# Output projection of a decoder trunk: six of eight tiles as three Strassen pairs with factors through DRAM, tiles 6 and 7 plain and last

## The chip, the cores and the metric

The kernel runs on one core of a Trainium2 chip. The core has five engines that run their own instruction streams and meet at semaphores: TensorE (PE in the profile; PEld is its weight load), VectorE (DVE), ScalarE (ACT), GpSimd (POOL) and SyncE (SP). SP, ACT and POOL also issue DMAs. Data lie in SBUF (128 partitions) and, for matmul results, in PSUM (eight banks of 128 x 512 floats). The metric is the device time of one execution in microseconds (us), the median of several runs.

## The reference

A sequence of 1024 positions with model width 1024 goes through one RG-LRU layer and one attention layer, both with a residual, and a final norm. The change lies in the end of the attention layer:

```
def mla_layer(x, norm_g, w_in, q_norm, w_uq, w_out, k_nope, k_rope, v, cos, sin):
    ...
    o = causal_block_attention(q_nope, q_rope, k_nope, k_rope, v)
    y = o.reshape(bsz, seq, N_HEADS * V_DIM) * jax.nn.silu(gate)
    return y @ w_out
...
x = x + mla_layer(...)
return rms_norm(x, final_norm)
```

There are 8 heads of 128 values, so `y` is 1024 x 1024 and `y @ w_out` is a product of two 1024 x 1024 matrices. Everything is float32.

## The kernel before

**Layout.** Activations lie transposed: 128 channels on the partitions, 1024 positions in the free dimension. A *page* is one such 128 x 1024 tile; a pool of 36 pages (`pgs`, `NPAGES`) serves nearly all large tiles, and an allocation waits until a page is free. A product in float32 accuracy is made of three matmuls on split operands: `hl` (lines 83 to 85) writes the high part on ACT and the remainder on DVE, and `mm3` (lines 115 to 118) issues high x high, high x low and low x high.

**Order.** The code is traced in program order and a list scheduler puts the instructions of each engine in order when the program is built, by priority and by what is ready in its model (`tc.high_priority` raises a block's priority). On the chip each engine then runs its stream strictly in that order.

**Strassen pairs that exist already.** The in-projection of the attention layer (`pair`, lines 628 to 667) multiplies two output tiles at a time in seven products of four k-pieces in place of eight (Strassen's scheme in Winograd's form), on factors of the activations that `factors` (line 510) makes and combinations of weight blocks from `wpair` (line 535). The last two of its pairs run just ahead of attention.

**Attention** (lines 989 to 1026) loops over 8 heads and, in each, 8 query blocks of 128 rows. `scores` (line 890) makes the scores of a block two blocks ahead (`LOOK`), with mask, row maximum (line 908), exponential (911), reciprocal (912) and, on DVE, the multiply by that reciprocal (913). `transposes` (916) turns the block's weights on PE and splits them. `pv` (927) multiplies four blocks with the values, multiplies the result with the gate on DVE (line 940) and splits it into the head's two pages `ysb`. For heads 0 to 5 (`NSPILL`) these pages are spilled to DRAM (line 946, GpSimd's DMA queue) and loaded again by `yload` during the last head. Between blocks, other work is put in by hand-written tables: key and query projections of the next head (`KQ_AT`), values (`V_AT`), and in the last head the first parts of the output projection (`D_AT`, `dpart`): tiles 0 and 1 for the first 512 columns and heads 0 to 5, 12 parts of three matmuls.

**Output projection and final norm** (lines 1034 to 1103). `wout` (960) loads the weights of a tile, high part by a casting DMA on GpSimd's queue and remainder on DVE. Then for each of three column chunks of 512, 256 and 256 (`CHUNKS`) the eight tiles follow one another, each with 24 matmuls (`mmt`), an addition of the residual from DRAM (`x1d`, line 1081), a square on ACT (1086) and its sum on DVE (151). After the second tile of the next chunk, `final` (1048) ends the chunk before: a matmul with ones sums the squares over partitions, `root` (1043) makes the reciprocal root, and DVE multiplies each tile by gain and root and sends it out. The last chunk gets its gains on ACT (1094) and ends with four DVE multiplies of two tiles each and four output DMAs (1100 to 1103).

Of the kernel before, what the change touches and what calls it, by code (L numbers as in the profile page):

```python
# [27 lines left out]
NSPILL = 6  # L28
WPRI = 100
WOUT_AT = (-1, 1, 2)  # L30
YL_AT = (0, 0, 0, 0, 1, 2)
DSTART = 0
DPART = tuple((dt, k, k + 1) for dt in range(2) for k in range(6))
# [6 lines left out]
D_AT = (0, 4, 1, 1, 1, 0, 3, 2)  # L40
# [7 lines left out]
FINAL = ((0, 2, "sync"), (2, 4, "scalar"), (4, 6, "sync"), (6, 8, "scalar"))  # L48
# [11 lines left out]
def trunk(tc, xT, wina, vecs, wgate, wouta, winc, wuk, wuv, wuq, wuqr, woutb, rope, outT):  # L60
# [746 lines left out]
    for j in range(0, NH, 2):  # L807
        gts = [[tk(), tk()] for _ in range(2)]
        w = wpair(6 + j, wa)
        if j < NH - 2:  # L810
            banks = four()
        else:

            pp.close()
            pss = es.enter_context(tc.tile_pool(name="pss", bufs=2, space=PSUM, reuse_waits="tile"))
            banks = [pss.tile([P, HW], F32, tag="pm", bufs=4, name=nm("pm")) for _ in range(4)]
# [16 lines left out]
    def pm():  # L833
        return pss.tile([P, HW], F32, tag="pm", bufs=4, name=nm("pm"))
# [55 lines left out]
    def scores(hd, qb, k, q, qs):  # L890
# [5 lines left out]
        sc = ps[:, o:o + nk]  # L896
        for c0, c1 in ((0, min(nk, HW - o)), (HW - o, nk)):
            if c0 >= c1:
                continue
            c = slice(c0, c1)  # L900
            T.matmul(out=sc[:, c], lhsT=q[0][:, ql], rhs=k[0][:, c], start=True, stop=False)  # L901
            T.matmul(out=sc[:, c], lhsT=q[0][:, ql], rhs=k[1][:, c], start=False, stop=False)  # L902
            T.matmul(out=sc[:, c], lhsT=q[1][:, ql], rhs=k[0][:, c], start=False, stop=False)  # L903
            T.matmul(out=sc[:, c], lhsT=qs[:, ql], rhs=R1[:, c], start=False, stop=False)  # L904
            T.matmul(out=sc[:, c], lhsT=qs[:, ql], rhs=R2[:, c], start=False, stop=True)  # L905
# [7 lines left out]
        V.tensor_scalar(out=p_[:, 0:nk], in0=p_[:, 0:nk], scalar1=l, scalar2=None, op0=ALU.mult)  # L913
# [13 lines left out]
    def pv(hd, g, pts):  # L927
# [13 lines left out]
        if g == 0:  # L941
            ysb[hd] = (page(), page())
        hl(y, ysb[hd][0][:, hs(g)], ysb[hd][1][:, hs(g)])
        if hd < NSPILL and g == 1:
            for i in range(2):
                DQ.dma_start(out=ysd[hd, i], in_=f(ysb[hd][i]))

    gates = []
    ysb = [None] * NH

    ysd = dp.tile([NSPILL, 2, P, S], F32, name="ysd")

    def yload(hd):
        ysb[hd] = (page(), page())
        for i in range(2):
# [73 lines left out]
    while dwork:  # L1029
        dwork.pop(0)()  # L1030
# [127 lines left out]
```

## Time and profile before

| | |
|---|---|
| median of 3 runs | 867.9 us (867.41 to 868.46) |
| the profiled execution | 867.47 us |
| its span, first to last instruction | 865.7 us |
| last attention matmul issued | 775.5 us after the span's start |
| last projection matmul done | 855.84 us |
| mean granted TensorE clock | 0.997 |

Times in rows of the profile are us from the span's start. A row of the timeline has start, duration, engine, line, operation, output <- input, shape. A row of the groups has line, engine, operation, shape and count, then the busy time in us and the mean in ns of one, then the idle time of the engine ahead of them and what ended it. A row of the windows has the stretch and then the busy time (and count) of PE, PEld, DVE, ACT and POOL, the granted clock, the busy share of the DMA engines and the GB/s that they moved. Matmuls overlap in a pipeline, so the distance of two starts tells their cost, not the duration of one.

### The profile page before, as it was taken

Reading aid. Unit: us, or ns where it says so; the run is one execution under the profiler, and the core shown is the slowest. Engines: PE = TensorE matmul, PEld = TensorE weight load, DVE = VectorE, ACT = ScalarE, POOL = GpSimd, SP = SyncE. Lnnn points to the kernel's source line nnn. Section 1 sums busy time; section 2 is a strip of 40 time slices with the busy share of each in tenths; the row PEclk is TensorE's granted clock in tenths of the full one; section 3 lists DMA queues with packets and bytes.
Section 4 is the critical chain, followed back from the end, with each engine's and each line's share of the span. In section 5 each row is a group of like instructions: output and inputs, shape, how many; then the busy total and the mean of one; then the engine's idle time right before and its main releaser. Section 6 shows DMA issues by size and latency. Waiting matters only on the chain.

```text
span 865.7 us, 12199 instructions
## 1 busy us (share of the span) xinstructions
PE 854.0 (99%) x4326; PEld 728.3 (84%) x4326; DVE 660.9 (76%) x1227; ACT 518.3 (60%) x961; POOL 73.6 (9%) x143
## 2 busy tenths in 40 slices
PE   9999999999999999999999999999999999999995
PEld 7788888888888888888888889888998898888995
DVE  7888778777877774779998957887897787775453
ACT  8557787777788542699876555555564555431222
POOL 1000110011000110100212320000000000010000
PEclk9999999999999999999999999999999999999998
DMA  8333333333213445133546673131231324866032
GB/s 300 93 97 101 96 96 98 110 94 99 77 42 92 157 147 176 50 105 114 177 140 204 216 255 113 53 98 76 77 113 62 123 63 148 335 213 205 21 127 73
DMA packets 52221, 109.00 MB, mean 126 GB/s; under 512 B 6592, under 2 KB 17216, under 8 KB 52160
## 3 DMA queue, kind: packets, MB, share of 16 engines
q1 hardware_dynamic: 36112, 67.05, 24.0%
q0 software_dynamic: 15216, 40.51, 14.0%
q8 instruction: 34, 0.56, 0.3%
q10 hardware_dynamic: 832, 0.66, 0.2%
q14 instruction: 27, 0.22, 0.1%
HBM read 81.46 MB, written 26.21 MB: 124 GB/s over the span
## 4 chain that ended last, share of the span: by engine, by line
PE 95%; DVE 2%; issue 1%; DMA 1%; ACT 1%; SPq 0%; DVEq 0%
PE ps L117 18%; PE ps L116 18%; PE ps L118 18%; PE pm L118 6%; PE pm L116 6%; PE pm L117 6%; PE pm L921 4%; PE pm L937 2%; PE pm L938 2%; PE s L904 2%; PE s L905 2%; PE s L903 2%; PE s L902 2%; PE s L901 2%; PE pm L936 2%
## 5 line engine op out<-in xcount | busy, mean ns | idle before, releaser
L117 PE MATMUL ps<-pg,wh 128*128 128x512 f32 x664 | 258.8, 390 | 0.5 <-DVE pg L255 0.4
L118 PE MATMUL ps<-pg,wl 128*128 128x512 f32 x664 | 258.4, 389 | 0.0
L116 PE MATMUL ps<-pg,wh 128*128 128x512 f32 x664 | 257.9, 389 | 0.0
L117 PEld LDWEIGHTS ps<-pg,wh 128*128 128x128 f32 x664 | 124.6, 188 | 27.6 <-DVE pg L255 1.9
L116 PEld LDWEIGHTS ps<-pg,wh 128*128 128x128 f32 x664 | 124.6, 188 | 26.5 <-DVE tk L656 0.3
L118 PEld LDWEIGHTS ps<-pg,wl 128*128 128x128 f32 x664 | 124.6, 188 | 25.8
L84 ACT ACTIVATE pt<-pm 128x512 fp32r<-128x512 f32 (+2 forms) x96 | 44.4, 490 | 58.1 <-PE pm L921 54.8
L911 ACT ACTIVATE pg<-s,m 128x128 f32<-128x128 f32 (+3 forms) x64 | 47.5, 743 | 47.1 <-DVE m L908 40.7
L116 PE MATMUL pm<-pg,pg 128*128 128x256 f32 (+1 forms) x192 | 61.9, 322 | 0.0
L117 PE MATMUL pm<-pg,pg 128*128 128x256 f32 (+1 forms) x192 | 61.6, 321 | 0.0
L118 PE MATMUL pm<-pg,pg 128*128 128x256 f32 (+1 forms) x192 | 61.3, 320 | 0.0
L85 DVE TENSOR_TENSOR pt<-pm,pt 128x512 fp32r<-128x512 f32 (+2 forms) x96 | 50.5, 549 | 3.2 <-ACT pt L84 3.2
L908 DVE TENSOR_REDUCE m<-s 128x1 f32<-128x128 f32 (+3 forms) x64 | 48.1, 753 | 1.2
L383 DVE SCALAR_TENSOR_TENSOR t<-xb,vec,t 128x512 f32<-128x512 f32 x60 | 44.8, 747 | 0.4
L84 ACT ACTIVATE pg<-pg 128x512 fp32r<-128x512 f32 x42 | 26.1, 632 | 29.4 <-DVE pg L437 18.0
L84 ACT ACTIVATE wh<-wr 128x512 fp32r<-128x512 f32 (+3 forms) x55 | 29.0, 531 | 24.5 <-PE ps L117 11.9
L921 PE MATMUL pm<-ident,pg 128*128 128x128 f32 x288 | 42.3, 274 | 0.0
L118 PE MATMUL pm<-pg,wl 128*128 128x512 f32 x108 | 42.3, 392 | 0.0
L117 PE MATMUL pm<-pg,wh 128*128 128x512 f32 x108 | 42.3, 392 | 0.0
L116 PE MATMUL pm<-pg,wh 128*128 128x512 f32 x108 | 42.2, 391 | 0.0
L85 DVE TENSOR_TENSOR wl<-wr,wh 128x512 fp32r<-128x512 f32 (+3 forms) x55 | 30.5, 566 | 14.3 <-ACT wh L84 14.1
L116 PEld LDWEIGHTS pm<-pg,pg 128*128 128x128 f32 x192 | 36.6, 191 | 2.7 <-issue 0.2
(232 smaller groups left out, 1807.5 us busy)
## 6 DMA issues: line engine op xcount, KB each, us to landing
wr<-wina SPq DMA_DIRECT2D x38, 256.0 KB, 2.8
wh<-wina POOLq DMA_DIRECT2D x36, 256.0 KB, 3.0
wa<-winc SPq DMA_DIRECT2D x24, 256.0 KB, 3.1
ysd<-pg POOLq DMA_DIRECT2D x12, 512.0 KB, 3.0
pg<-ysd SPq DMA_DIRECT2D x12, 512.0 KB, 9.8
wr<-wouta SPq DMA_DIRECT2D x16, 256.0 KB, 2.7
t<-xT SPq DMA_DIRECT2D x16, 256.0 KB, 3.4
x1d<-t POOLq DMA_DIRECT2D x16, 256.0 KB, 2.5
```

Of the source, the lines that this page charges most:

```text
L84: A.activation(out=hi, in_=src, func=AF.Copy)
L85: V.tensor_tensor(out=lo, in0=src, in1=f(hi), op=ALU.subtract)
L116: T.matmul(out=ps, lhsT=w[0], rhs=r[0], start=first, stop=False, skip_group_check=more)
L117: T.matmul(out=ps, lhsT=w[0], rhs=r[1], start=False, stop=False, skip_group_check=more)
L118: T.matmul(out=ps, lhsT=w[1], rhs=r[0], start=False, stop=last, skip_group_check=more)
L383: V.scalar_tensor_tensor(out=xc, in0=xb[:, j:j + HW], scalar=cwv[j], in1=xc, op0=ALU.mult, op1=ALU.add)
L901: T.matmul(out=sc[:, c], lhsT=q[0][:, ql], rhs=k[0][:, c], start=True, stop=False)
L902: T.matmul(out=sc[:, c], lhsT=q[0][:, ql], rhs=k[1][:, c], start=False, stop=False)
L903: T.matmul(out=sc[:, c], lhsT=q[1][:, ql], rhs=k[0][:, c], start=False, stop=False)
L908: V.tensor_reduce(out=m, in_=sc, axis=AX.X, op=ALU.max, negate=True)
L911: A.activation(out=p_[:, 0:nk], in_=sc, func=AF.Exp, bias=m, accum_out=l)
L921: T.transpose(out=ps[:, (b - b0) * P:(b - b0 + 1) * P], in_=p_[:, b * P:(b + 1) * P], identity=ident)
```

## The change

**Output projection.** Tiles 0 to 5 are now computed as three pairs (0, 1), (2, 3), (4, 5). The sum over k is halved (heads 0 to 3 and 4 to 7), the columns are halved (512 and 512), and each pair takes seven products `f0` to `f6` of four pieces (`mm3` each, 512 columns) in place of eight. `outpair` gives the pieces; partial results are passed between four PSUM banks by ACT copies (a negated to b, later b to d), subtracted from the residual (`less`) or added to it (`put`), and squared (`addsq`). `opair` loads two weight tiles as pages and makes seven split weight combinations, step by step as a generator, so that for the first pair the steps are spread over the last head (`OP_AT`); they share the pool's four buffers for high and low parts.

**Factors of y.** `pv` no longer splits `y` itself. `yfactors` makes pieces of work that the loop takes one per block (`ywork`): for heads 0 to 3 the two halves and their difference; for heads 4 to 7 five factors, from the half blocks and the earlier head's difference, which goes through DRAM (`tbd`). Each factor is a page with high and low part of 512 columns. Those of heads 0 to 5 are spilled to DRAM (`fyd`) and loaded again in the last head (`F_AT`) and after it (`yget`).

**Last head.** Its filler work is now 14 pieces of the first pair (`f0`, `f1` whole, three of `f4`, three of `f2`). When all scores are made, the score banks are closed and become four banks `psd` for the pairs. The scores of block 6 of the last head write the full bank width.

**Softmax multiply.** In heads 4 to 7 (`PNORM`) the multiply by the reciprocal is an ACT Copy with scale in place of the DVE multiply.

**Tiles 6 and 7 and the end.** They are computed plainly, last, in the same three chunks; their right-hand sides are the factors 0, 4, 7 and 6, which are the plain halves of `y`. The gains of all tiles are now multiplied in on ACT (`gains`). The final multiplies of a chunk run under the next chunk's tiles: for the first chunk three tiles on GpSimd, one on DVE and two pairs on DVE; for the second two on GpSimd and three pairs on DVE; for the last two single tiles and three pairs on DVE.

```
+PNORM = 4
+OP_AT = (1, 2, 0, 0, 1, 0, 2, 0)
+F_AT = (((0, 0), (0, 1), (0, 2), (0, 3)), ((1, 0), (1, 1)), ((1, 2), (1, 3)), (), ((4, 0), (4, 1)), ((2, 0), (2, 1)), (), ())
+D_AT = (0, 4, 1, 1, 1, 1, 3, 3)
...
+            c = slice(c0, S if (hd, qb) == (NH - 1, 6) and c1 == nk else c1)
...
-        V.tensor_scalar(out=p_[:, 0:nk], in0=p_[:, 0:nk], scalar1=l, scalar2=None, op0=ALU.mult)
+        if hd < PNORM:
+            V.tensor_scalar(out=p_[:, 0:nk], in0=p_[:, 0:nk], scalar1=l, scalar2=None, op0=ALU.mult)
+        else:
+            A.activation(out=p_[:, 0:nk], in_=p_[:, 0:nk], func=AF.Copy, scale=l)
...
+    def yput(i, j, src, spill):
+        pg = page()
+        hl(src, pg[:, hs(0)], pg[:, hs(1)])
+        if spill:
+            DQ.dma_start(out=fyd[i, j], in_=f(pg))
+        else:
+            fy[i][j] = pg
...
+        if g == 0:
+            return [lambda: yput(0 if hd < 4 else 4, j, y0, spill)]
+        if hd < 4:
+            def t1():
+                diff(y0, y0, y1)
+                yput(1, j, y0, True)
+                DQ.dma_start(out=tbd[j], in_=gates[hd])
+            return [lambda: yput(7, j, y1, True), t1]
+        t1, b12 = halves(tb[hd])
...
+        return [lambda: put(2, t1, y1, t1, ALU.add), lambda: put(3, b12, b12, y1),
+                lambda: yput(6, j, y1, spill), lambda: put(5, y0, y0, t1)]
...
+    def rest(op, done):
+        run(op["f2"][done:])
+        op["mid"]()
+        run(op["f4"][done:])
+        run(op["f3"])
+        op["p22"]()
+        op["p11"]()
+        run(op["f6"])
+        op["p12"]()
+        run(op["f5"])
+        op["p21"]()
...
+        for d in range(2):
+            (V if c.stop == S else G).tensor_tensor(out=x2[d][:, c], in0=x2[d][:, c], in1=r, op=ALU.mult)
+            (nc.sync, nc.scalar if c.stop == S else nc.sync)[d].dma_start(out=outT[d, :, c], in_=x2[d][:, c])
+        if c.start == 0:
+            G.tensor_tensor(out=x2[2][:, c], in0=x2[2][:, c], in1=r, op=ALU.mult)
...
+            V.tensor_tensor(out=x2[3][:, c], in0=x2[3][:, c], in1=r, op=ALU.mult)
...
+        for d in range(2 if c.start == 0 else 0, 6, 2):
+            x = x2a[:, d:d + 2, c]
+            V.tensor_tensor(out=x, in0=x, in1=r.unsqueeze(1).to_broadcast([P, 2, n]), op=ALU.mult)
```

More of the change, by code (lines that the diff above doesn't have):

```diff
@@ L1046, in root @@
         newton(out, ps, 1.0 / D, t1, t2)
[L1048 to L1056 removed]
+    acc = [td.tile([P, HW], F32, tag="acc", name=nm("acc")) for _ in range(2)]
```

332 lines of the change are left out of this document (230 added, 102 removed).

## The prediction

> **What bounds the kernel now.** I read the page's busy times, its chain, then what TensorE (PE) waits for, then the two stages that the change touches.
>
> ```profile
> PE 854.0 (99%) x4326; PEld 728.3 (84%) x4326; DVE 660.9 (76%) x1227; ACT 518.3 (60%) x961; POOL 73.6 (9%) x143
> PE 95%; DVE 2%; issue 1%; DMA 1%; ACT 1%; SPq 0%; DVEq 0%
> PE pm L1090 <- ACT sq L1086: 0.5, 1, 0.5
> PE s L901 <- ACT pg L911: 0.4, 1, 0.4
> ```
>
> The first line is busy time by engine, the second the chain that ended last, the other two all that PE waits for from 513 us on: 0.9 us. So the end is set by the number of matmuls and by what follows the last one. A busy PE alone proves little, since ends are modelled; the starts say more.
>
> ```profile
> 775.86 0.40 PE L117 MATMUL pm<-pg,pg 128*128 128x512 f32 x1
> 779.95 0.39 PE L117 MATMUL pm<-pg,pg 128*128 128x512 f32 x1
> 848.08 0.28 PE L116 MATMUL pm<-pg,pg 128*128 128x256 f32 x1
> 855.28 0.28 PE L116 MATMUL pm<-pg,pg 128*128 128x256 f32 x1
> L116 PE MATMUL pm<-pg,pg 128*128 128x256 f32 x128 | 36.8, 288 | 0.0
> L116 PE MATMUL pm<-pg,pg 128*128 128x512 f32 x48 | 18.7, 390 | 0.0
> ```
>
> Between the first two rows lie 18 matmul steps: 4.09/18 = 0.227 us for one of 512 columns. Between the next two lie 60: 7.20/60 = 0.120 us for one of 256, slightly over half. The last two rows count one of the three lines of a product, from the last attention matmul (775.58) to the end; all three give 144 and 384. 144 x 0.227 + 384 x 0.120 = 78.8 us, and with the ones-matmuls nearly the 80.3 us up to 855.84: the stage is matmuls at pitch, with no hole.
>
> **The matmuls removed.** The projection has 8 tiles x 8 k x 3 = 192 products per column half. Before: 192 of 512 columns (chunk 0, of which 48 run before 775.58) and 384 of 256. After: three pairs x 7 products x 4 pieces x 3 = 252 of 512; tiles 6 and 7 keep 48 of 512 and 96 of 256. So 288 of 256 go, 108 of 512 come:
>
> -288 x 0.120 + 108 x 0.227 = -34.6 + 24.5 = **-10.0 us**.
>
> All of it lies on the path, for PE waits for nothing else there.
>
> **The widened score** of the last head's block 6: five matmuls of 384 columns become 512.
>
> ```profile
> 756.32 0.40 PE L905 MATMUL s<-pg,qs 128*128 128x512 f32 x1
> 756.55 0.34 PE L901 MATMUL s<-pg,pg 128*128 128x384 f32 x1
> 756.73 0.34 PE L902 MATMUL s<-pg,pg 128*128 128x384 f32 x1
> ```
>
> Steps of 0.23 and 0.18: 5 x 0.05 = **+0.3 us**, on PE.
>
> **Attention, DVE and ACT.** One head (661.2 to 692.1):
>
> ```profile
> 661.20:692.10 30.90, 30.90 (x187) 27.63 (x186) 25.75 (x57) 17.04 (x40) 1.07 (x2) 1.00 0.26 86
> L913 DVE TENSOR_SCALAR pg<-pg,l 128x640 f32<-128x640 f32 (+7 forms) x8 | 4.1, 518 | 0.2
> L85 DVE TENSOR_TENSOR pg<-pg,pg 128x512 fp32r<-128x512 f32 x2 | 1.4, 683 | 0.0
> L84 ACT ACTIVATE pg<-pg 128x512 fp32r<-128x512 f32 x2 | 1.3, 634 | 0.3 <-DVE pg L940 0.3
> L1094 ACT ACTIVATE pg<-pg,fn 128x256 f32<-128x256 f32 x8 | 4.1, 510 | 0.2
> L1086 ACT ACTIVATE sq<-x 128x512 f32<-128x512 f32 x7 | 4.4, 633 | 23.8 <-DVE x L1081 23.8
> L1086 ACT ACTIVATE sq<-x 128x256 f32<-128x256 f32 x7 | 2.9, 418 | 15.6 <-DVE x L1081 15.6
> ```
>
> The first row has PE, PEld, DVE, ACT, POOL busy, then clock, DMA share, GB/s. A split is 0.68 on DVE and 0.63 on ACT; a difference is an SBUF tensor_tensor of 512, priced like the split's DVE half. Heads 0 to 3 get three splits and one difference where there were two splits: DVE 25.75 + 1.4 = 27.1 of 30.9, ACT +0.6. Heads 4 to 7 get three splits and three differences more (DVE +4.1, ACT +1.9), and the softmax multiply leaves DVE (-4.1) for ACT. No row has that ACT form at 1024 columns; L1094 is the same form at 256 (0.510), and the squares give (633-418)/256 = 0.84 ns per column. Mean width 576: 0.51 + 320 x 0.00084 = 0.78 us, 6.2 per head, against DVE's 0.52 each. So DVE stays at 25.8 and ACT goes to 17.0 + 6.2 + 1.9 = 25.1 of 30.9: no engine overtakes PE. What matters is whether a row is ready before its transposes.
>
> ```profile
> 676.34 0.74 DVE L913 TENSOR_SCALAR pg<-pg,l 128x1024 f32<-128x1024 f32 x1
> 677.29 0.98 ACT L84 ACTIVATE pt<-pm 128x512 fp32r<-128x512 f32 x2
> 678.65 0.97 PE pm L921 x8
> 661.53 0.55 DVE L913 TENSOR_SCALAR pg<-pg,l 128x640 f32<-128x640 f32 x1
> 670.33 0.57 PE pm L921 x5
> ```
>
> The widest row is ready at 677.08, 1.6 us before its transposes; that of 640 has over 8 us. On ACT the widest takes 0.51 + 768 x 0.00084 = 1.15, 0.4 longer, and fits; but evictions queued behind it (L84, here 0.95 us later) move back by up to a microsecond, and PE's transposes wait for their banks. I take 0.25 us per head of 4 to 7, **+1.0 us**; ends 0 (slack and four banks cover it) and 11.5 (below). For DVE in heads 0 to 3 I take nothing: in the gate stage, itself Strassen pairs, DVE is full and PE still issues at pitch.
>
> ```profile
> 480.00:490.00 10.00, 10.00 (x46) 8.29 (x45) 9.98 (x17) 5.96 (x11) 3.26 (x7) 1.00 0.51 175
> 785.00:795.00 10.00, 10.00 (x46) 8.29 (x45) 4.68 (x8) 1.90 (x3) 0.00 (x0) 1.00 0.85 265
> L946 POOL DMA_DIRECT2D ysd<-pg x12 | 6.4, 535 | 197.1 <-ACT pg L84 192.7 <-DVE pg L913 2.9 <-DVE pg L85 1.5
> pg<-ysd SPq DMA_DIRECT2D x12, 512.0 KB, 9.8
> ```
>
> That row also covers the new pairs: the same 46 matmuls per 10 us as the plain stage, with copies, seven weight splits and four additions per pair (pair total here: 11 DVE operations plus ten on outputs, about 14 us under 84 x 0.227 = 19.1 of PE). I cost the pairs' own waits at 0, ends 0 and 3 (one late copy or split per pair, about 1 us).
>
> **Queues.** POOL issues 26 spills of 512 KB for 12 (0.535 each, spread over six heads; nothing urgent is behind them until the weight casts of tiles 6 and 7). SP issues 26 page loads (four of them `tbd`) for 12, but six weight loads of 512 KB and two tiles' raws replace eight tiles' raws. In head 7 each load waits for a free page, and SP's later ones wait behind it: the x1 loads, then factors 3, 6, 5. By my count of live pages the pool just holds (35 of 36 at block 5 of head 7; the q, k and rope pages go after the last scores, near 763 us). At 2.0 us each (512 KB at the 265 GB/s of the 785:795 row) the queue from there is x1 twice, factor 3 twice (in by 771, used near 780), the next weights, factor 6 twice (779, used near 782), factor 5 twice (783, used near 785). Cost 0; exposed, up to 4.
>
> **Hand-over from attention to projection.** Before, the matmuls behind the last `pv` don't need its result for over 30 us. Now the next piece, the fourth of product 2, needs head 7's second half through y, a sum and a split.
>
> ```profile
> 775.47 0.27 PE L938 MATMUL pm<-pt,pg 128*128 128x128 f32 x1
> 777.08 0.68 DVE L940 TENSOR_TENSOR pg<-pm,pg 128x512 f32<-128x512 f32 x1
> 777.80 0.64 ACT L84 ACTIVATE pg<-pg 128x512 fp32r<-128x512 f32 x1 [7.34 <-DVE pg L940]
> 779.64 0.68 DVE L85 TENSOR_TENSOR pg<-pg,pg 128x512 fp32r<-128x512 f32 x1
> ```
>
> 0.68 + 0.68 + 0.64 + 0.68 = 2.7, with semaphores 3.0 us from 775.7 to the next matmul. Cover: the last piece of product 4 (3 x 0.227 = 0.7), and, if their pages and weights are there, three of product 6 (2.0) or the next pair's first. All of PE's later matmuls stand behind the wait. That the order on PE isn't the code's is seen above: 48 - 36 = 12 matmuls from behind the last `pv` ran ahead of it. I take half the chain, **+1.5 us** (ends 0 and 3.7, the chain plus the copy of b into d).
>
> **Tail.** Now 855.84 to 865.7:
>
> ```profile
> 855.84 0.42 DVE L1081 TENSOR_TENSOR pg<-pm,pg 128x256 f32<-128x256 f32 x1 [1.54 <-PE pm L118]
> 858.36 0.42 DVE L143 SCALAR_TENSOR_TENSOR t<-pm,t 128x256 f32<-128x256 f32 x1 [2.10 <-ACT t L142]
> 859.36 2.50 DVE L1102 TENSOR_TENSOR pg<-pg,acc 128x512 f32<-128x512 f32 x4
> L161 POOL TENSOR_SCALAR_AFFINE_SELECT mask<-mask 128x128 f32<-128x128 f32 x1 | 0.3, 289 | 0.0
> masks.py:199 POOL TENSOR_SCALAR_AFFINE_SELECT ident<-ident 128x128 f32<-128x128 f32 x1 | 0.3, 327 | 0.0
> ```
>
> Last multiplies: two of 256 and three pairs for four pairs, 2 x 0.42 + 3 x 0.6 = 2.6 for 2.5: +0.1. But chunks 1 and 2 shrink from 64 x 3 x 0.120 = 23 us to 5.8 each, and the multiplies of the chunk before must fit under them. On DVE from chunk 1's start: roots 1.4 + 0.85, multiplies 0.7 + 2 x 1.2 and 3 x 0.7, additions and sums 3.0, in all 10.4 us, startable after about 3 us of a 12.9 us stretch. A backlog of about 1 us meets the 2.1 us that DVE idles in the tail anyway. I take +0.6 for an operation in the way of the last addition and square, so **+0.7**; ends 0.1 and 4. A GpSimd (POOL) multiply has no row: nearest are DVE's own 0.69 for 512 and POOL's 0.327 for 128 columns, times four 1.3. I take 1.3: 3 x 1.3 + 2 x 0.65 = 5.2 us, done about when the last matmul ends.
>
> The Trainium skill speaks against this (SBUF — State Buffer, Who interferes with whom): a DVE instruction with two SBUF inputs and a GpSimd instruction that reads SBUF exclude each other, the second waiting for all of the first. No run here shows it, since before has no POOL arithmetic. By that rule the sum would be that of rival D below.
>
> **Sum.** 867.47 (profiled execution: span 865.7 and 1.8 around it; 0.4 under the median 867.9) - 10.0 + 0.3 + 1.0 + 1.5 + 0.7 = **861.0 us**.
>
> **Rivals.**
> - A, the forecast, 859 to 863: 0.50.
> - B, the ACT multiply sets the pace of heads 4 to 7. Each block then takes longer by 0.78 - 0.52 plus a hop of 0.1 between engines, 0.36 us; 32 blocks: 11.5 us in place of 1.0, so 871.5. It decides once blocks lose over 0.3 us each (the gain of 10 less the other terms is then gone). For it: the widest row has only 1.6 us of slack, and ACT would be at 81%. Against: PE lost nothing with DVE at 83%. 0.12.
> - C, the pages: factor loads wait for the last scores and come late to products 3, 6 and 5, the hand-over has no cover: +3.7 - 1.5 and up to +4: 864 to 867, say 865. For: 35 of 36 pages. 0.14.
> - D, POOL and DVE multiplies shut each other out near the end: DVE's 10.4 + 5.2 us don't fit the 12.9, 2.7 over, less what the idle 2.1 absorbs: +1 to +2.7, 863. 0.12.
> - E, every new wait is covered: 867.47 - 10.0 + 0.3 + 0.1 = 857.9. For: PE has no wait anywhere near now. 0.12.
>
> A measurement of this kernel tells 0.2% (1.7 us) from no change. Faster: A, D, E and most of C, 0.83; the same: the far end of C or a weak B, 0.06; slower: B, 0.11. The range takes E's end less half a microsecond and C's whole: 857.3 to 867.0.
>
> **What would show it.** In the changed profile: 252 + 48 = 300 projection matmuls of 512 columns and 96 of 256, at 0.227 and 0.120. PE's waits: one of 1 to 2 us for DVE at the hand-over; under 0.3 us per head at the transposes of heads 4 to 7, on ACT. The last matmul near 849, the tail near 10.5 us. Wrong if PE waits for ACT or DVE in every block (B), for DMA after 776 (C), or if DVE multiplies take longer than 0.69 or wait beside POOL's (D).

## The result: 875.9 us, and the profile after

The changed kernel takes 875.93 us (median of 5 executions, 875.44 to 876.86) against 867.9: a ratio of 1.0093, 95% interval 1.0082 to 1.0104. It is **8 us slower**, where 861.0 was forecast. A few executions are disturbed and far longer (950 to 3030 us where the others of the same kernels take 864 to 880); the medians leave them out, and no times of PE are read where the profiled execution was one of them (run 1 and the third of run 5).

The page and the waits of PE from 513 us on (in total, times, longest), of the changed kernel; the lines answer to the first four of the prediction:

```profile
PE 850.3 (97%) x4146; PEld 714.4 (82%) x4146; DVE 679.2 (78%) x1234; ACT 566.7 (65%) x1046; POOL 85.8 (10%) x156
PE 84%; DVE 7%; ACT 4%; issue 2%; DMA 1%; POOL 0%; SPq 0%; DVEq 0%; POOLq 0%; ACTq 0%
```

```profile
PE pm L1313 <- DVE acc L151: 2.5, 1, 2.5
PE s L905 <- ACT pg L915: 1.9, 2, 1.4
PE pd L117 <- DVE pg L85: 1.6, 1, 1.6
PE pm L928 <- DVE pt L85: 1.4, 1, 1.4
PE pd L116 <- ACT pg L84: 1.3, 1, 1.3
PE pm L1314 <- ACT sq L1046: 1.2, 1, 1.2
PE pm L928 <- DVE pg L85: 0.8, 3, 0.3
PE pm L116 <- ACT pd L1067: 0.7, 1, 0.7
```

PE has 180 matmuls fewer and is still on the ending chain, but DVE and ACT now hold 11% of it. Its waits grew from 0.9 to 11.4 us, and they are few and long: eight of over 0.4 us. The borders of the stages are starts of PE's rows, of which these are the last attention matmul, the last projection matmul and the two ones-matmuls of the last root:

```profile
783.07 0.27 PE L945 MATMUL pm<-pt,pg 128*128 128x128 f32 x1
...
859.75 0.28 PE L118 MATMUL pm<-pg,pg 128*128 128x256 f32 x1
862.50 0.70 PE L1313 MATMUL pm<-acc,onesd 128*128 128x256 f32 x2 [2.47 <-DVE acc L151]
864.41 1.22 PE L1314 MATMUL pm<-sq,onesd 128*128 128x256 f32 x2 [1.22 <-ACT sq L1046]
```

"At pitch" is the sum of the steps that the matmuls of a stage take when nothing holds them (0.227 us for 512 columns, 0.120 for 256, and so on); what is over that is called holes.

| stage (us) | before | after | difference | of it at pitch | of it holes |
|---|---|---|---|---|---|
| to the first score matmul | 522.14 | 523.69 | +1.55 | the same code | +1.55 |
| attention, to the last `pv` matmul | 253.33 | 259.38 | +6.05 | -0.9 | +6.95 |
| projection, to its last matmul | 80.05 | 76.68 | -3.37 | -8.9 | +5.53 |
| end, to the end of the span | 10.18 | 14.15 | +3.97 | | +3.97 |
| span | 865.7 | 873.9 | +8.2 | -9.8 | +18.0 |

(The -0.9 are five filler matmuls that no longer fall ahead of the last `pv` matmul, less the five widened scores.) So the matmuls went as forecast, but the holes are nearly twice as much, and most of them lie in three places: the last head, the hand-over behind it, and the end.

**The last head.** Head by head (from one head's last `pv` matmul to the next's), and against the kernel before, heads 0 to 3 have 1.1 us of new holes together, heads 4 to 6 have 0.5 to 0.6 each and head 7 has 4.2. Two places make most of head 7's. First ACT and then PE, at 753 us:

```profile
753.53 0.63 ACT L84 ACTIVATE wh<-ws 128x512 fp32r<-128x512 f32 x1 [4.38 <-DVE ws L1007]
...
754.33 0.68 ACT L915 ACTIVATE pg<-s,m 128x512 f32<-128x512 f32 x1
```

```profile
755.15 0.50 PE L905 MATMUL s<-pg,pg 128*128 128x512 f32 x1 [1.38 <-ACT pg L915]
...
771.62 0.55 PE L928 MATMUL pm<-ident,pg 128*128 128x128 f32 x3 [1.39 <-DVE pt L85]
```

On ACT a weight split of the first pair (`wh<-ws`) is next in line and waits 4.4 us for DVE to add its weights; the exponential behind it, whose score bank PE wants, starts only after it. At 770 PE has run out of filler: its transposes wait for a bank, and the next pieces, those of product 4, write to bank a, which must first be copied to bank b; that is one of the score banks, which come free only with the last exponential (`PE pm L116 <- ACT pd L1067`, 0.7 us).

**The hand-over.** DVE behind the last attention matmul, then PE:

```profile
783.38 0.69 DVE L947 TENSOR_TENSOR pg<-pm,pg 128x512 f32<-128x512 f32 x1 [3.87 <-PE pm L945]
783.99 0.16 DVE L1201 TENSOR_SCALAR fn<-vec 128x8 f32<-128x8 f32 x1
784.05 0.68 DVE L1087 TENSOR_TENSOR pg<-pm,pg 128x512 f32<-128x512 f32 x1
784.66 1.89 DVE L978 TENSOR_TENSOR pg<-pg,pg 128x512 f32<-128x512 f32 x3
786.46 0.69 DVE L1007 TENSOR_TENSOR ws<-pg 128x512 f32<-128x512 f32 x1
787.06 0.69 DVE L85 TENSOR_TENSOR wl<-pg,wh 128x512 fp32r<-128x512 f32 x1
787.66 1.89 DVE L85 TENSOR_TENSOR pg<-pg,pg 128x512 fp32r<-128x512 f32 x3
```

```profile
786.10 0.50 PE L116 MATMUL pd<-pg,wh 128*128 128x512 f32 x1 [1.34 <-ACT pg L84]
...
788.40 0.50 PE L117 MATMUL pd<-pg,wh 128*128 128x512 f32 x1 [1.57 <-DVE pg L85]
...
789.96 0.63 PE L118 MATMUL pm<-pg,wl 128*128 128x512 f32 x1
790.38 0.63 PE L116 MATMUL pm<-pg,wh 128*128 128x512 f32 x1
...
792.85 0.39 PE L118 MATMUL pd<-pg,wl 128*128 128x512 f32 x1
```

Between y (L947) and the low part of product 2's factor (the first L85 of 787.66) stand seven other operations: a constant, an output addition, three factor differences of which only one is needed first, and two weight operations of the second pair. The chain takes 5 us from 783.4 to 788.4. Then matmuls follow each other at about 0.43 us in place of 0.227 (789.96 to 790.38) for 3.3 us, up to 792.5; the rows of the windows show the granted clock, 0.73 in the second stretch:

```profile
785.00:790.00 5.00, 2.33 (x8) 1.56 (x9) 5.00 (x9) 3.28 (x6) 0.00 (x0) 0.93 0.39 124
790.00:795.00 5.00, 5.00 (x18) 4.00 (x17) 1.70 (x4) 0.63 (x2) 0.00 (x0) 0.73 1.01 391
```

**The end.** GpSimd (POOL) and DVE, from the first half's root on:

```profile
854.89 3.04 POOL L1281 TENSOR_TENSOR pg<-pg,acc 128x512 f32<-128x512 f32 x2 [32.29 <-DVE acc L144]
857.89 2.27 POOL L1284 TENSOR_TENSOR x2a<-x2a,acc 128x512 f32<-128x512 f32 x1
860.52 2.50 POOL L1281 TENSOR_TENSOR pg<-pg,acc 128x256 f32<-128x256 f32 x2 [0.36 <-DVE acc L144]
```

```profile
855.00 1.77 DVE L1286 TENSOR_TENSOR x2a<-x2a,acc 128x512 f32<-128x512 f32 x1
856.70 2.32 DVE L1290 TENSOR_TENSOR x2a<-x2a,acc 128x1024 f32<-128x1024 f32 x1
...
859.27 0.41 DVE L1309 TENSOR_TENSOR x2a<-pm,x2a 128x256 f32<-128x256 f32 x1
859.60 0.85 DVE L144 SCALAR_TENSOR_TENSOR acc<-t,t 128x256 f32<-128x256 f32 x1
860.37 1.21 DVE L1290 TENSOR_TENSOR x2a<-x2a,acc 128x1024 f32<-128x1024 f32 x1
861.50 0.94 DVE L151 TENSOR_TENSOR acc<-acc,sq 128x256 f32<-128x256 f32 x1
```

Beside POOL a DVE multiply of 512 with both inputs in SBUF takes 1.77 us, one of 1024 2.32, a sum of 256 0.94. The same operations without POOL beside them take 0.69, 1.21 and 0.43. Those with one input in PSUM (`pm`) keep their 0.41 throughout. The last sum (861.50) is therefore late, and PE's last ones-matmuls wait 2.5 us for it.

### The profile page after: what moved, and what is told of

Its sections match the earlier page's. It is cut to its first block, busy times and chain, and to the rows that moved or that the text cites. A ratio compares the mean times of both kernels' runs of the same rounds, so it can differ in the third digit from the quotient of the medians.

```text
span 873.9 us, 11947 instructions
## 1 busy us (share of the span) xinstructions
PE 850.3 (97%) x4146; PEld 714.4 (82%) x4146; DVE 679.2 (78%) x1234; ACT 566.7 (65%) x1046; POOL 85.8 (10%) x156
## 4 chain that ended last, share of the span: by engine, by line
PE 84%; DVE 7%; ACT 4%; issue 2%; DMA 1%; POOL 0%; SPq 0%; DVEq 0%; POOLq 0%; ACTq 0%
PE ps L116 17%; PE ps L117 17%; PE ps L118 17%; PE pm L116 4%; PE pm L118 4%; PE pm L117 4%; PE pm L928 2%; PE pm L945 2%; PE pm L944 2%; PE pm L943 2%; PE s L905 2%; PE s L906 2%; PE s L907 2%; PE s L909 2%; PE s L908 2%
## 5 line engine op out<-in xcount | busy, mean ns | idle before, releaser
L116 PE MATMUL ps<-pg,wh 128*128 128x512 f32 x664 | 258.0, 390 | 0.6 <-ACT pg L254 0.4
L116 PEld LDWEIGHTS ps<-pg,wh 128*128 128x128 f32 x664 | 124.5, 188 | 27.7 <-ACT pg L254 0.8
L116 PE MATMUL pm<-pg,wh 128*128 128x512 f32 x140 | 55.3, 395 | 0.7 <-ACT pd L1067 0.7
L85 DVE TENSOR_TENSOR pt<-pm,pt 128x512 fp32r<-128x512 f32 (+2 forms) x96 | 50.6, 550 | 6.4 <-ACT pt L84 6.0
L117 PE MATMUL pm<-pg,wh 128*128 128x512 f32 x140 | 55.1, 393 | 0.0
L118 PE MATMUL pm<-pg,wl 128*128 128x512 f32 x140 | 55.1, 393 | 0.0
L84 ACT ACTIVATE pg<-pg 128x512 fp32r<-128x512 f32 x58 | 35.8, 628 | 19.1 <-DVE pg L437 17.9
L85 DVE TENSOR_TENSOR wl<-wr,wh 128x512 fp32r<-128x512 f32 (+3 forms) x55 | 30.9, 566 | 14.3 <-ACT wh L84 14.0
L85 DVE TENSOR_TENSOR pg<-pg,pg 128x512 fp32r<-128x512 f32 x58 | 39.2, 686 | 2.5 <-ACT pg L84 2.2
L928 PEld LDWEIGHTS pm<-ident,pg 128*128 128x128 f32 x288 | 33.2, 140 | 8.6 <-DVE pt L85 2.9
L905 PE MATMUL s<-pg,pg 128*128 128x512 f32 (+2 forms) x96 | 37.1, 386 | 1.9 <-ACT pg L915 1.9
L99 POOL DMA_DIRECT2D wh<-wina x36 | 19.3, 536 | 180.2 <-PE ps L118 160.6
```

Of the source, the lines that this page charges most:

```text
L84: A.activation(out=hi, in_=src, func=AF.Copy)
L85: V.tensor_tensor(out=lo, in0=src, in1=f(hi), op=ALU.subtract)
L99: G.dma_start(out=hi, in_=src)
L116: T.matmul(out=ps, lhsT=w[0], rhs=r[0], start=first, stop=False, skip_group_check=more)
L117: T.matmul(out=ps, lhsT=w[0], rhs=r[1], start=False, stop=False, skip_group_check=more)
L118: T.matmul(out=ps, lhsT=w[1], rhs=r[0], start=False, stop=last, skip_group_check=more)
```

## The experiments

All are compared with the kernel before, timed alongside on the same chip (867.7 to 868.2). The theory at the start: **three separate costs**, namely the lock between POOL and DVE at the end, the chain at the hand-over, and the work on DVE and ACT in head 7. The rivals: the prediction's B (ACT's multiply), and that the costs are one, a DVE that is full.

**1. The last multiplies on DVE.**

```diff
-(V if c.stop == S else G).tensor_tensor(out=x2[d][:, c], in0=x2[d][:, c], in1=r, op=ALU.mult)
+V.tensor_tensor(out=x2[d][:, c], in0=x2[d][:, c], in1=r, op=ALU.mult)
```

(and the same for `x2[2]`.)

> Edit: the five final multiplies that GpSimd makes go to DVE, nothing else. Theory L (GpSimd and DVE shut each other out): in the changed kernel a DVE multiply of 512 columns took 1.77 us beside GpSimd and 0.69 elsewhere. Without GpSimd it is 0.69 again, pairs of 512 take 1.2, and the stretch from the last projection matmul to the end shrinks from 14.0 us by 2 to 3.5: 872.4 to 874 us. Rival B (DVE simply has too much work at the end): DVE gets 3 x 0.69 + 2 x 0.42 = 2.9 us more, the end grows by 1 to 3: 877 to 879 us.

871.7, ratio 1.0046 (1.0029 to 1.0063): some 4 us gained by giving DVE five more operations, though its three executions lie between 870.8 and 873.7. (Later expectations take 3.2 us from this run, by a median of 872.69 over all four of its executions.) DVE's multiplies of 512 and 1024 are back at 0.68 and 1.22 in its profile. The lock at the end is confirmed; two traces size it better: with this edit the end, 14.15 us in the changed kernel, is 11.76 in run 5's first kernel, and run 7 has 11.71 without POOL and 14.29 with it.

**2. The softmax multiply, on DVE in all heads and on ACT in all heads.**

```diff
-PNORM = 4
+PNORM = 8      (and, in the other kernel, 0)
```

> Edit: the softmax multiply stays on DVE in all heads (PNORM 8). Theory A (the ACT multiply costs PE its waits in heads 4 to 7): heads 4 to 6 give back some 1.5 us and part of the 4.4 us of head 7: 872 to 874.5 us, and PE's waits for ACT's exponential go. Rival S (DVE is what is full, with the factors): DVE gets 4.1 us more per head, waits grow, 878 us or more. No change within 0.7 us would say that neither engine's share of this work sets the waits.

> The changed kernel with the softmax's multiply on ScalarE in all eight heads (in the changed kernel heads 0 to 3 have it on VectorE). Theory: VectorE is what is full in the attention; with the multiply of heads 4 to 7 put back on it the run lost 2.2 us and the attention's waits rose from 6.1 to 8.95, so taking it off in heads 0 to 3 gains what those heads still wait, about 0.9: 874.5 to 875.5. Rival (the second of the prediction's): ScalarE's multiply stands between the exponential and the transposes and sets the pace where it is used, so four heads more of it cost 1 us or more: 877 or above.

878.13 (1.0117, 1.0102 to 1.0132) and 877.0 (1.0103, 1.0086 to 1.0119): 2.2 and 1.1 us above the changed kernel, whose own ratio is known to 0.1% either way. The first speaks against B; the second missed its theory's number and just reaches the rival's. One row of PE's waits decides. In the changed kernel it has 0.8 us in three waits, one each in heads 4, 5 and 6; with DVE's multiply everywhere it is gone; with ACT's everywhere it has one wait in each of heads 0 to 6:

```profile
PE pm L928 <- DVE pg L85: 1.9, 7, 0.3
```

The lengths of the heads agree, which hold the same matmuls in all four kernels: heads 1 to 3 take 30.99 us each before, 31.31, 31.31 and 31.11 in the changed kernel and 31.60 each with ACT's multiply; heads 4 and 5 take 31.61 and 31.62 with ACT's and 31.31 and 31.43 with DVE's. So ACT's multiply costs about 0.3 us per head, near what the sum took for it and far from B's 2.9, and doesn't set the pace. A further 0.1 to 0.4 per head comes with the factors, whichever engine multiplies.

Head 7 has 4.2 us of new holes in the changed kernel, 6.6 with the multiply on DVE, and 5.7 with ACT's in all heads, where its own code is that of the changed kernel. In this last kernel its three stops are those of the changed kernel to 0.01 us; what is new is a stretch of slow matmuls behind them, which the changed kernel's profiled execution doesn't have there (its granted clock is 1.00 in these windows):

```profile
770.00:775.00 5.00, 2.96 (x14) 2.19 (x13) 3.47 (x7) 4.84 (x10) 0.00 (x0) 0.81 0.92 335
775.00:780.00 5.00, 5.00 (x24) 4.07 (x24) 1.82 (x4) 1.27 (x3) 0.00 (x0) 0.85 1.03 417
```

The kernel with DVE's multiply has the same stretch (0.80 and 0.86), besides longer stops. So the second kernel's 1.5 us more in head 7 are the clock's in that execution and not the multiply's, and so is a good part of the first kernel's 2.4.

**3. The hand-over, three ways.** In the first, the fourth piece of product 2 reads the third's factor (tiles 0 and 1 change); in the second, DVE keeps the written order for y's factors and the rest of the splits; in the third, the last piece of product 2 comes late and goes into both banks.

```diff
-            pg = fy[i][j]
+            pg = fy[i][2 if (m, f_, j) == (0, 2, 3) else j]
```

```diff
+    with tc.manual_schedule(engines={_E.DVE}):
         while ywork:
             ywork.pop(0)()
         for _ in left:
             pass
```

```diff
-        run(op["f2"][done:])
-        op["mid"]()
+            op["copyd"]()
             run(op["f4"][done:])
+            run(op["f3"][:3])
+            run(op["f2"][done:])
+            op["f2d"]()
```

> Edit: the fourth piece of product 2 of the first pair reads the third piece's factor in place of its own, so it doesn't wait for the last head's second half; the output of tiles 0 and 1 is changed by it. Theory H (the hand-over chain through DVE and ACT holds PE for 2.9 us, and the pause brings the slow clock that costs 1.4 to 2 us more): both go, 870.5 to 872 us, and no matmul pitch of 0.43 us remains after 783 us. Rival P (factor pages loaded late hold PE there anyway): a wait for DMA takes its place, 875 us or more. If only the wait goes and product 3's factor is late next, 873 to 874.

> Edit: at the hand-over DVE keeps the code's order among head 7's last factors and the remaining weight splits, so the low part of product 2's factor is the 5th DVE operation behind y and not the 8th. Theory H2 (the wait of 2.9 us is DVE operations queued ahead of that low part, not the chain's own length): the low part is ready about 1.8 us earlier, the second wait (1.6 us) goes, and with a shorter pause the slow clock may not come (1.4 us more): 872.5 to 874.3 us. Rival (the chain itself is too long, whatever the order): within 0.7 us of 875.9.

> Edit: in the first pair the copy of b into d is made before the last piece of product 2, which then goes into both banks: 3 matmuls more (0.7 us), but three pieces of products 3 and 6 each stand free to run behind the last attention matmul (18 matmuls, 4.1 us). The result is the same sum. Theory H: PE has no wait over 0.5 us at the hand-over and the clock stays full: 4.4 (what the dependency alone cost) less 0.7: 872 to 872.8 us. Rival P (pages of products 3 and 6 late): 875 us or more, PE waits for DMA.

871.3 (1.0034, 1.0022 to 1.0047), 872.27 (1.005, 1.0035 to 1.0064) and 871.3 (1.004, 1.0025 to 1.0055): 4.6, 3.7 and 4.6 us gained. In the first and the third the projection's holes fall from 5.5 to 1.1 and 1.2. In the second the wait of 1.34 stays and the one of 1.57 is gone, and with it the slow matmuls. The hand-over is confirmed. Of its 5.5 us some 1.6 (eight steps of 0.2) were the slow pace behind the second wait.

**4. Head 7's weight splits.** First spread over more blocks, then five of the seven left out.

```diff
-OP_AT = (1, 2, 0, 0, 1, 0, 2, 0)
+OP_AT = (1, 1, 0, 1, 1, 1, 1, 0)
```

```diff
         split(a11)
         yield
+        if m == 0:
+            split(a12)
+            out.extend(out[n % 2] for n in range(5))
+            return
```

> Edit: the weight combinations of the first pair spread one to a block over the last head, (1,1,0,1,1,1,1,0) for (1,2,0,0,1,0,2,0). Theory Q (weight splits queued on DVE and ACT in front of a block's maximum and exponential hold PE in head 7, 1.5 us at 753 and 2.4 us at 769 to 773): 1 to 3 us less, 873 to 875 us. Rival: the engines are full in any order in head 7 and the waits only move, within 0.7 us of 875.9.

> The changed kernel, but of the first pair's seven weight combinations only two are made (the split of a11 and that of a12) and each is used for several products: four additions and five splits on VectorE and five copies on ScalarE are left out, tiles 0 and 1 of the output change, and everything else is as it was. Theory: head 7's stalls of about 4.4 us come from VectorE, which has the weight splits beside the softmax and the factors, so with nine of its operations gone (about 6.2 us of 0.68 each, some five of them in head 7) at least 2.5 us of the 4.4 go; besides, the low part of product 2's last factor comes four operations earlier after the last attention matmul, which takes away the second wait of the hand-over (1.6 us) and the slow matmuls behind it (about 1.5): together 875.9 - 2.5 - 3.1 = 870.3. Rival: the stalls come from the factors of heads 6 and 7 and the order of the filler on TensorE, so head 7 keeps about 4 us, and only the hand-over gains: 872.8.

875.18 (1.0088, 1.0071 to 1.0105): nothing that can be told. 877.19 (1.011, 1.0093 to 1.0127): slower, where both theories had a gain. PE's rows of the second kernel:

```profile
752.47 0.50 PE L905 MATMUL s<-pg,pg 128*128 128x512 f32 x1 [0.44 <-ACT pg L915]
...
768.73 0.98 PE L928 MATMUL pm<-ident,pg 128*128 128x128 f32 x7 [1.39 <-DVE pt L85]
...
785.48 0.50 PE L116 MATMUL pd<-pg,wh 128*128 128x512 f32 x1 [3.62 <-ACT pg L84]
```

The wait at the exponential falls from 1.38 to 0.44, so that one was the split in front of it on ACT; the one for a transpose bank stays, so that one was not. And the first wait of the hand-over grows from 1.34 to 3.62: with the first pair's splits gone, the scheduler put the second pair's in their place, a split on ACT in front of the factor's. That is the hand-over's theory once more, but as a test of head 7 the total says nothing: head 7's new holes are 3.0 for 4.2, and the projection's 8.7 for 5.5, with a slow stretch twice as long behind the longer wait (granted clock 0.62 and 0.70 from 785 to 795).

**5. The edits together.** Runs 1, 3 (second and third) and 4 (first) in one kernel; the same with tiles 4 and 5 plain; and runs 1 and 3 (third) alone.

```diff
-    for k, m in enumerate((2, 4)):
+    for k, m in enumerate((2,)):
```

> Edit: the final multiplies on DVE, the weight steps spread, the ordered chain and the cover together. If the losses lie in separate places they add: 875.9 - 3.2 - 0.7 - 3.7 = 868.3, 867.3 to 869.3 us. If one cause (DVE load) moves from place to place: 870 us or more.

> Edit: as the one before, but only tiles 0 to 3 as Strassen pairs; 4 to 7 plain, so each 256-column chunk has 96 matmuls (11.5 us) to lie over the multiplies of the chunk before. PE gets 12 x 0.227 = 2.7 us more and some more for 256-wide ones (96 of 256 for 48 of 512: 0.6). Theory T (the end is late since two tiles per chunk are too short a cover for DVE): the end after the last projection matmul goes back to about 10 us, some 1.5 to 3 less than in the run with multiplies on DVE, so 867.5 to 870.5 us in all, within 1.5 us of the run before. Rival (cover doesn't matter): the full 3.3 us slower than the run before.

> Two edits put on the changed kernel together: the last multiplies that GpSimd made go to VectorE, and the last piece of the first pair's product 2 (the one with head 7's factor) is put off by copying the bank before it and is then added to both banks (three more matmuls). Theory: the end and the hand-over are separate costs, so the gains add: 875.9 - 3.2 - 4.6 = 868.1, ratio about 1.000 against the kernel before. Of the matmuls about 9.3 us are gained, and what is left to pay is head 7's stalls (about 4 us), those of heads 0 to 6 (about 2), the end (about 1) and a start that came out about 1.5 us later. Rival: the kernel that had these two edits with two more (the order on VectorE and the spread weight splits) came out at 870.5, and if the shortfall there comes from the ends not adding, this one is at 870 to 871 too; if it came from the ordered VectorE chain, this one is faster than that one by 1.5 to 2.5 us.

870.51 (1.0029, 1.0019 to 1.0039), 875.61 (1.0089, 1.0074 to 1.0104), 870.0 (1.0019, 1.001 to 1.0029). The gains don't add up: sums of 868.3 and 868.1 were expected of the first and the third. The trace of the first shows what is left, against the kernel before: head 7 keeps 4.1 us; the projection keeps 2.6, 1.06 of it a new wait, since the written order pushes the split of product 5's weights back; and the end keeps 1.6, for DVE is busy from 856.4 to 860.3 with the last addition and then the multiplies of the column group before, and only then begins the last root. In the third, single executions lie between 868.0 and 871.2; what tells them apart is open. Two pairs are slower than three by 5.1, more than even the rival's 3.3. The end does go back, to 10.6 us, as the theory had it; but PE waits 2.4 us at 815.7 for an addition that stands on DVE behind a late weight load, and head 7 has a slow stretch as in run 2. So the third pair pays, by less than 5.1.

**6. The plain tiles ahead.** What the last head needs as filler is work that asks nothing of DVE and ACT, and what the hand-over needs is matmuls without head 7's factors. The plain tiles' first half is the one, products 0 and 1 are the other. The order is turned round:

```diff
-            dwork = op["f0"] + op["f1"] + op["f4"][:3] + op["f2"][:3]
+            dwork = [lambda a=a: dpart(*a) for a in DPART]
...
+    def dpart(dt, k):
+        if k == 0:
+            ahead[dt] = pm()
+        pg = fy[0 if k < 4 else 4][k % 4]
+        mm3(ahead[dt], wob[dt][k], (pg[:, hs(0)], pg[:, hs(1)]), k == 0, k == NKT - 1)
...
-    for c0, n in CHUNKS:
+    for c0, n in CHUNKS[1:]:
```

> All the work of the changed kernel in another order: the first half of the columns of the plain tiles 6 and 7 is what fills the last head (16 pieces of three matmuls, the same number as before less none), their weights are split on VectorE in heads 6 and 7 (four operations, no ScalarE), only two splits of the first pair are made in head 7, all three pairs follow after the attention, starting with products 0 and 1, which need no factor of head 7 (24 matmuls, 5.4 us, in front of the first product that does), and the plain tiles' second half comes last; the last multiplies are all on VectorE. Theory: the matmul count is the same, so against 875.9 go the hand-over (5.4 us, with the slow matmuls), the multiplies on GpSimd (3.2), about 2 of head 7's stalls, and about 1 more at the end, since the first half's root no longer stands beside the plain matmuls of the same half: 875.9 - 11.6 = 864.3, ratio 0.996 against the kernel before. Rival: the ten pages that are read after the last head come too late for the products, which now use them sooner, or the weights of tiles 6 and 7 come late in head 7: new waits of 3 to 6 us on a load, 867.5 to 870.

868.92 (1.0015, 1.0005 to 1.0024): a miss by 4.6 us. It lies in the rival's range, but not by the rival's mechanism: PE waits for no load. Head 7's new holes fall from 4.2 to 0.9 and no wait over 0.5 us is left in it. But PE now waits behind the last head:

```profile
794.15 0.50 PE L117 MATMUL pd<-pg,wh 128*128 128x512 f32 x1 [1.64 <-ACT wh L85]
```

```profile
783.34 0.58 ACT L1068 ACTIVATE pd<-pd 128x512 f32<-128x512 f32 x1 [5.53 <-PE pd L119]
783.84 0.62 ACT L85 ACTIVATE pg<-pg 128x512 fp32r<-128x512 f32 x1
```

The copy of product 0's bank stands on ACT in front of the first factor's split and waits 5.5 us for PE; all of the chain moves back. Two more steps: the order of DVE and ACT written out, then the residual of tiles 0 and 1 in the buffer that is free at once, that of 6 and 7 in pages.

```diff
+    with tc.manual_schedule(engines={_E.DVE, _E.Activation}):
+        ywork.pop(0)()
+        next(left)
+        op["neg"]()
+        next(left)
+        next(left)
+        for _ in range(3):
+            ywork.pop(0)()
```

```diff
-    op = outpair(0, w0, pdb, pdb, (pdb, lambda: page(F32)))
+    op = outpair(0, w0, pdb, pdb, (pdb, lambda: x2a[:, next(n2), :]))
...
-                x2[dt] = x2a[:, dt - 2, :]
+                x2[dt] = page(F32)
```

> The kernel with the plain tiles' first half ahead, with the order on VectorE and ScalarE written out between the last attention matmul and the first pair's third product: the factor of product 2, then the weights of product 2, then the copy of the bank (which stood first on ScalarE and held the factor back for 2.7 us), then the weights of products 3 and 4, then the other factors. Theory: in the kernel before this one 0.6 us of wait at 785.6, 2.0 at 792.1 and about 1.9 of matmuls at half pace behind it came from this order alone, so 868.9 - 4.5 = 864.4, ratio 0.996 to 0.997 against the kernel before. Rival: the additions of tiles 6 and 7, which stand on VectorE in the middle of this list, wait for their loads until the queue is empty (in the trace of the kernel before this one it moved 413 GB/s from 780 to 787.5), and the fifth weights come late again: 866 to 867.

> The kernel with the plain tiles ahead and the written-out order, and the softmax's multiply on ScalarE in all heads. Theory: the two edits touch different stages, so this is the sum: 864.4 - 0.5 to 1 = 863.5 to 864, ratio 0.995 to 0.996. Rival: as for the run with the multiply alone: 865.5 or above, slower than without it.

> The kernel with the plain tiles ahead and the written-out order, with the places of two buffers exchanged: the residual of tiles 0 and 1 lies in the buffer that is free when the last head's work is over, and that of tiles 6 and 7, needed at the end, in the pages, which come free later. Theory: in the run before, TensorE did not wait at all after the last attention matmul (779.2) until 792.9 and then waited 3.7 us for product 6, because the residual of tile 1 had to be taken from that product's bank first and its page was loaded from 790.7 on; with the load at 779.5 that wait goes, and with it the slow matmuls that follow such a pause in some of the executions: 868.3 (that run's profiled execution) - 3.8 = 864.5, with less spread between the executions; ratio 0.996. Rival: the second pair's weights, which are read into the next pages to come free, are then what is late, at the start of that pair (798): a wait of 1.5 to 3 us, 866 to 867.5.

The first step alone gives 870.77 (1.0039, 1.0025 to 1.0053), a miss, and with the multiply on ACT 872.83 (1.0055, 1.0042 to 1.0068), 2.1 us more, as that run's rival had it. The profiled execution of the first, 868.32, is the fastest of its five. In it PE does not wait at all for 13.8 us behind the last attention matmul, and then for one thing, which neither theory had named. PE, the queue of SP and DVE of the first of these kernels:

```profile
797.05 0.47 PE L117 MATMUL pd<-pg,wh 128*128 128x512 f32 x1 [3.73 <-issue]
```

```profile
790.67 1.68 SPq L1059 DMA_DIRECT2D pg<-x1d  x2
```

```profile
796.26 0.69 DVE L1080 TENSOR_TENSOR pg<-pd,pg 128x512 f32<-128x512 f32 x1 [0.41 <-DMA pg<-x1d]
```

Product 6 adds to a bank that DVE must read first, with tile 1's residual, whose page came free at 790.67 and was filled by 796. With the second step this wait is gone: **864.25 us, ratio 0.9961 (0.9948 to 0.9975)**, where 864.5 was expected. These are all of PE's waits in that kernel from 513 us on, beside the 11.4 us above:

```profile
PE s L906 <- ACT pg L916: 0.9, 2, 0.5
PE pm L929 <- DVE pg L86: 0.8, 3, 0.3
PE pm L1328 <- ACT sq L1047: 0.3, 1, 0.3
```

Against the kernel before, this trace still has 3.7 us of new holes in the attention (2.8 in heads 0 to 6, which the order doesn't touch), 0.9 in the projection, an end 1.5 us longer and a start 0.3 later: 6.4 of the 9.8 that the matmuls save.

**7. GpSimd in that kernel.** Four of its multiplies go back to POOL.

> The same kernel with the multiplies of tiles 6 and 7 of the first two column groups on GpSimd (four operations), which in this order lie beside plain matmuls, with the last root further away than in the changed kernel. Theory: GpSimd's multiplies slow VectorE's operations on two SBUF inputs wherever they lie beside each other (0.69 to 1.77 us in the changed kernel), but only VectorE's work in front of the last root counts; here two of the four (the second group's) are near it, so the cost is 0.5 to 1.5 us: 865 to 866 where the kernel without it is at 864.5. Rival: the multiplies on GpSimd take work off VectorE, which is what stands in front of the last root, so the end is the same or up to 1 us shorter: 863.5 to 864.5.

866.9 (0.9992, 0.9983 to 1.0001): 2.65 us slower, more than the theory's 0.5 to 1.5, and the end grows from 11.71 to 14.29. The same group without POOL, then with it:

```profile
L1302 DVE TENSOR_TENSOR x2a<-x2a,acc 128x1024 f32<-128x1024 f32 x3 | 3.7, 1217 | 0.0
```

```profile
L1302 DVE TENSOR_TENSOR x2a<-x2a,acc 128x1024 f32<-128x1024 f32 x3 | 5.8, 1943 | 0.0
```

The multiplies of the column group before stand in DVE's order ahead of the last additions, so even there the lock reaches the last root.

## Why the prediction was wrong

| term of the sum | forecast | measured |
|---|---|---|
| matmuls, with the widened score | -9.7 | -9.8 |
| waits in the attention | +1.0 | +6.9 |
| hand-over | +1.5 | +5.5 |
| end | +0.7 | +4.0 |
| the stretch up to the first score | 0 | +1.55 |

- **The matmuls: right.** The groups of the changed kernel from the last attention matmul on, one of the three lines of a product each, count 96 of 256 columns and 48 of 512 for the plain tiles:

```profile
L116 PE MATMUL pm<-pg,pg 128*128 128x256 f32 x32 | 9.0, 282 | 0.0
L116 PE MATMUL pm<-pg,pg 128*128 128x512 f32 x16 | 6.2, 389 | 0.0
```

- **The pairs' own waits at 0, pages and queues at 0: right for this kernel.** From 793 us to the last root's sum PE waits for nothing, and nowhere for a load. The page rival (C) came true only in another order (run 6, first step), where a page came free late for a residual.
- **The attention: the step that failed is the one that summed busy time per head and asked only whether a row is ready before its transposes.** It priced head 7's splits and factors as load on DVE and ACT (27 of 31 us, no engine full) and did not ask what stands behind each of them in an engine's order. One split that waits for its input holds the exponential behind it, and filler that needs a score bank is no filler while scores are made. The first is shown by the wait that falls from 1.38 to 0.44 when that split goes. For the second there is only that the waits of 770 to 773 are absent in all five kernels with other filler (runs 6 and 7), which differ in more than that. Heads 0 to 6 lose the other 2.8 us: ACT's multiply (B's cause) about 0.3 in each head that has it, near the 0.25 of the sum, and 0.1 to 0.4 per head that come with the factors and stay with DVE's multiply, where the sum had nothing. What makes these, and the rest of head 6's, wasn't sought.
- **The hand-over: right in kind, too small in size.** The chain was summed from its own four operations, 3.0 us, and half of it taken as covered. It is 5.0 long, as other operations stand between them on DVE, and the pause brought a slow stretch of PE that the sum had no term for. The upper end, 3.7, was below the 5.5 measured.
- **The end: rival D, priced at 1 to 2.7 and given 0.12, came true beside the forecast's own term; together they are 4.0.** The prediction's sign for D was seen: DVE multiplies longer than 0.69, waiting beside POOL's. The lock is 2.4 to 2.6 of the 4.0 (14.15 against 11.76 in run 5's first kernel, 14.29 against 11.71 in run 7). The other 1.5 stays without POOL: multiplies of the column group before stand on DVE ahead of the last root, where the sum had +0.6. The 1.3 taken for a POOL multiply of 512 was near: its rows of 1.5 to 2.3 hold its own waits for DVE, and the first of them is about 1.2 without them (an estimate: of DVE's 1.77 beside it 0.69 are its own, so 1.08 are waiting, and POOL began 0.11 sooner). What failed is that the sum let the two run side by side. The Trainium skill's rule (SBUF — State Buffer, Who interferes with whom) is borne out here in both its halves: operations with two SBUF inputs are held, 0.69 against 1.77 us, those with one PSUM input are not, 0.41 beside POOL and 0.42 without. It stood in the prediction as a rival and should have been in the sum.
- **The start: most likely no effect of the change.** The code is the same; 1.1 of the 1.55 us arise within the first 12 us and the rest at 427 us. In the traces of the other kernels, with the same code there, the first score lies anywhere between 521.97 and 523.49, against 522.14 before. One trace per kernel doesn't settle it.

The chances followed: every way in which the forecast could turn to slower was put into one mechanism (B), and three small losses that each needed no luck were not added up.

## What to carry to other kernels

Where matmuls run without a hole, count what a change adds in front of each instruction in the strict order of the engines that feed PE, not only how full these engines are; filler for a busy stretch must be work that takes no bank and no engine of that stretch. After a switch from one stage to the next, put work first that needs nothing of the last results, and place buffers so that what comes free first holds what is needed first. Don't share two-input SBUF work between DVE and GpSimd near the end: here it made both slower. And before a difference of a microsecond or two between two traces is put down to an edit, compare their granted clocks stage by stage: one slow stretch is worth 1.5.

## What the runs showed of the hardware

- **Half pace after short pauses, in some executions only.** Two waits of 1.3 and 1.6 us within 4 us were followed by 3.3 us of matmuls at 0.43 in place of 0.227. The Trainium skill (TensorE: Matmul & The Clock Gate, Part 1) has the clock fall to half after an idle window of some 3.4 us and rise after a busy one; pace and length agree, but no single pause here was that long. Nor is it certain. Head 7's two stops of 1.39 and 0.66 us brought such a stretch in the profiled executions of run 2's second kernel and run 3's first, and none in the changed kernel's or in those of run 3's other two, with the same stops. After a pause of 3.7 us in the profile of run 6's first step the matmuls went on at full pace, after one of 3.6 in its sister kernel with ACT's multiply they did not.
- **GpSimd beside DVE gains nothing.** A POOL multiply of 512 columns took 1.5 us on average in one pair and 2.27 beside DVE's of 1024, their waits for each other included. From 854.9 to 860.4 the two engines made multiplies of six times 512 columns between them (three on POOL) and three short operations; at DVE's own 1.22 per 1024 and 0.42 that would be 6 x 0.61 + 3 x 0.42 = 4.9 us for DVE alone (an estimate), and it took 5.5.
